# Stored factors staged in a weight slot, four plain pairs per stage, and the first squares summed by POOL in a residual block kernel

## The chip, the cores and the metric

One program runs on one core of one Trainium2 chip. The metric is device microseconds for one execution; the median over the executions shown is compared. The engines that matter are PE (TensorE, matmuls, with PEld its weight loads), DVE (VectorE), ACT (ScalarE), POOL (GpSimd) and SP (SyncE), whose queue issues the DMAs in order.

## What is computed

```python
def reference(x, ...):
    x = x + 0.5 * swiglu(rmsnorm(x, norm_ffn1), ffn1_wg, ffn1_wu, ffn1_wd)
    h = rmsnorm(x, norm_mix)
    x_m, z_m, x_r, y_r = split(h @ w_in)
    out_m = mlstm_group(x_m, z_m, ...)      # 4 heads, chunkwise matrix memory
    out_r = rglru_group(x_r, y_r, ...)      # 4 block-diagonal groups, conv and scan
    x = x + concat[rmsnorm(out_m), rmsnorm(out_r)] @ w_out
    x = x + 0.5 * swiglu(rmsnorm(x, norm_ffn2), ffn2_wg, ffn2_wu, ffn2_wd)
    return rmsnorm(x, norm_final)

def swiglu(x, wg, wu, wd):
    return (silu(x @ wg) * (x @ wu)) @ wd
```

There are 1024 tokens and 1024 channels, the inner width of each SwiGLU is 2816 (22 rows of 128), and everything is float32.

## The kernel before

Tokens lie along the free dimension, channels along the 128 partitions. x is transposed: eight row tiles of 128 channels by 1024 tokens, each in two halves of 512 tokens. Every matmul operand is split into a high and a low part (`split`: a cast by ACT, line 111, and a subtraction by DVE, line 112), and each product is made of three matmuls (high by high, high by low, low by high), so one 128-deep step on 512 tokens is three matmuls of 512 columns.

**The two FFN stages** (`ffn`) bear the change. Each has 22 pairs of a gate row and an up row. The first `PLAIN` = 3 pairs are computed plainly: `plain(h, f)` makes, for one half of the tokens, 24 matmuls for the gate and 24 for the up product, so a pair costs 96 over both halves. They read `hT`, the split but not yet normalized x. From pair 3 on, a pair is one object `Pair`, which forms a two by two block product with seven block products of 12 matmuls each (84 in all), the last of them from the tile `wd`. That scheme needs sums of weight blocks (`Pair.sums`, POOL, lines 520 to 523) and sums of blocks of normalized x (`Mixed`: `normalize` line 381, `combine` line 388, `operand`). The seven factors B11, T1, T2, B21, T3, B22, T4 are split tiles called `bop`. `Mixed` is a list of fifteen steps, one of which is popped after each half of a `plain`; what is left is popped when a product asks for it.

The down projection uses the same scheme for rows 0 to 15 of the inner width: two groups of eight rows, each with seven `Stored` factors which `Sink` wrote to DRAM (`f_d`) while the gate and up pairs ran, and four `Pair`s per group. So the factors change twice in a stage: from the last gate and up pair to group 0, and from the last pair of group 0 to group 1. The last pair before such a change makes the next factors ready: `after(i)`, called behind block product i, calls `Stored.get` for factor i (two loads of 512 KB into `raw` tiles, two splits) and then `Pair.prepare(i)` for the next pair (loads, sums, splits). Rows 16 to 21 are multiplied plainly at the end.

**Buffers.** `rawp` has four tiles of 4 KB per partition for what comes from DRAM; a pair before the change holds four of them (g, u, s, z). `wup` has four slots of 8 KB per partition with the tag `wu` for split weights; a pair holds three (wg, ws, wz), and its fourth product operand wu lies in `wd`. `bigp` has six tiles for hT, x and the last four factors; `bx` has three for the first three factors. In an FFN stage the eight PSUM banks are one pool `B`. `rb_late` holds the reciprocal root of the mean square of each token, spread over all partitions; its last use in a stage is in the plain pairs and in `normalize`.

**The start.** Before the first FFN, for each half and row, x is loaded (SP), split and scaled into hT by ACT and DVE (lines 115 and 116), and squared. The squares of one row are summed over channels by PE: `square_on_pe` squares into a `t2` tile (ACT, line 248) and adds four float32 matmuls of two columns (line 250, eight records) to a PSUM bank. `rstd_of` makes the root (POOL, line 144), and `spread` (line 175 on PE, from tiles that DVE makes in line 172) puts it into `rb_late`. In the second FFN the last products of the output projection feed `Norm.feed`, where the squares are summed by POOL (line 187), with DVE for the last row, and `row_rstd` (line 152) sums over partitions on PE.

**Order.** The order on the engines is that of the program text, except that the tile framework issues an instruction once its buffers are free. What is to come later is written with `defer(n, fn)`: `fn` runs at the n-th `tick`, and there is a tick behind each `project_half`, each `project_halves`, each group of `products` and each block product. The plain part of an FFN runs in the order (half, pair): (0,0), (0,1), (1,0), then their finishes, (1,1), the first gate and up pair's loads, sums and two splits, (0,2), finishes, (1,2), two more splits.

## Time and profile before

| what | value |
|---|---|
| median of 3 runs | 2184.8 us (2182.94 to 2188.53) |
| the profiled execution, its own time | 2185.25 us |
| its span, first to last instruction | 2183.5 us |
| PE busy | 2095.9 us (96%) |
| DVE, ACT, POOL busy | 1230.9, 872.5, 735.6 us |
| share of the chain that ended last: PE, DVE, DMA, POOL | 74%, 10%, 6%, 4% |

PE is busy nearly throughout, but the busy time of a matmul is no measure of its rate: a matmul of 512 columns is shown as some 390 ns long while the next one starts 227 ns later. What is lost is therefore read from how many matmuls start in a stretch, and from the idle time in front of a matmul with its releaser in the brackets.

### The profile page before, as it was taken

Reading aid. Unit: us, or ns where it says so; the run is one execution under the profiler, and the core shown is the slowest. Engines: PE = TensorE matmul, PEld = TensorE weight load, DVE = VectorE, ACT = ScalarE, POOL = GpSimd, SP = SyncE. Lnnn points to the kernel's source line nnn. Section 1 sums busy time; section 2 is a strip of 40 time slices with the busy share of each in tenths; the row PEclk is TensorE's granted clock in tenths of the full one; section 3 lists DMA queues with packets and bytes.
Section 4 is the critical chain, followed back from the end, with each engine's and each line's share of the span. In section 5 each row is a group of like instructions: output and inputs, shape, how many; then the busy total and the mean of one; then the engine's idle time right before and its main releaser. Section 6 shows DMA issues by size and latency. Waiting matters only on the chain.

```text
span 2183.5 us, 25040 instructions
## 1 busy us (share of the span) xinstructions
PE 2095.9 (96%) x9618; PEld 1727.3 (79%) x9618; DVE 1230.9 (56%) x1682; ACT 872.5 (40%) x1183; POOL 735.6 (34%) x496
## 2 busy tenths in 40 slices
PE   8989999999899999999999999998999999989898
PEld 7778888877688788878778888776788888867687
DVE  4853333355663545675537998878733333365654
ACT  4343333342432345564546554233433333342333
POOL 1355555323222302232311122423554554233303
PEclk9999999999999999999999999998999999999999
DMA  3243222243442312122146332121433322253432
GB/s 137 77 172 108 102 102 105 78 169 101 164 157 72 122 39 68 65 90 103 68 144 223 106 107 71 56 98 47 144 131 101 107 102 101 88 172 104 138 106 78
DMA packets 98368, 236.08 MB, mean 108 GB/s; under 512 B 9412, under 2 KB 28100, under 8 KB 97224
## 3 DMA queue, kind: packets, MB, share of 16 engines
q1 hardware_dynamic: 98248, 234.48, 31.5%
q8 instruction: 75, 1.23, 0.2%
q14 instruction: 45, 0.37, 0.1%
HBM read 168.89 MB, written 65.55 MB: 107 GB/s over the span
## 4 chain that ended last, share of the span: by engine, by line
PE 74%; DVE 10%; DMA 6%; POOL 4%; ACT 3%; issue 3%; SPq 0%; POOLq 0%; DVEq 0%; ACTq 0%
PE bank_b L445 39%; PE bank_a L327 12%; PE bank_b L344 8%; PE bank_s L344 3%; PE bank_b L327 2%; DVE bop L112 2%; PE bank_a L893 2%; PE bank_b L320 2%; DVE wu L112 1%; PE bank_s L1170 1%; PE bank_b L1199 1%; DMA raw<-in_db_dram 1%; DVE xs L1324 1%; DMA raw<-f_d0B 1%; DMA raw<-f_d1B 1%
## 5 line engine op out<-in xcount | busy, mean ns | idle before, releaser
L445 PE MATMUL bank_b<-bop,wu 128*128 128x512 f32 x3888 | 902.5, 392 | 30.4 <-DVE xs L642 12.8
L445 PEld LDWEIGHTS bank_b<-bop,wu 128*128 128x128 f32 x3888 | 733.7, 189 | 190.4 <-issue 11.0
L112 DVE TENSOR_TENSOR wu<-raw,wu 128x1024 fp32r<-128x1024 f32 (+1 forms) x233 | 297.4, 1278 | 425.9 <-ACT wu L111 425.8
L111 ACT CAST wu<-raw 128x1024 fp32r<-128x1024 f32 (+1 forms) x233 | 242.9, 1046 | 378.7 <-PE bank_b L445 230.0
L327 PE MATMUL bank_a<-hT,wu 128*128 128x512 f32 x1488 | 345.7, 391 | 3.1 <-ACT t L921 1.4
L327 PEld LDWEIGHTS bank_a<-hT,wu 128*128 128x128 f32 x1488 | 277.9, 188 | 64.1 <-POOL hT L112 1.9
L520 POOL TENSOR_TENSOR raw<-raw 128x512 f32<-128x512 f32 x54 | 76.4, 1415 | 517.6 <-DMA raw<-in_up_dram 292.4
L445 PE MATMUL bank_b<-bop,wd 128*128 128x512 f32 x648 | 159.6, 394 | 11.1 <-DVE ct L614 4.4
L344 PE MATMUL bank_b<-u,wu 128*128 128x512 f32 (+1 forms) x768 | 162.6, 364 | 1.5 <-DVE xs L1324 0.8
L610 ACT COPY ct<-bank_b 128x512 f32<-128x512 f32 x114 | 67.0, 587 | 230.3 <-PE bank_b L445 230.3
L445 PEld LDWEIGHTS bank_b<-bop,wd 128*128 128x128 f32 x648 | 121.9, 189 | 40.8 <-issue 5.4
L344 PEld LDWEIGHTS bank_b<-u,wu 128*128 128x128 f32 x768 | 131.8, 189 | 26.6 <-DVE xs L1324 2.5
L327 PE MATMUL bank_b<-hT,wu 128*128 128x512 f32 x528 | 124.9, 395 | 4.2 <-DVE wu L112 2.5
L614 DVE TENSOR_TENSOR ct<-ct,bank_b 128x512 f32<-128x512 f32 x114 | 78.0, 684 | 83.0 <-PE bank_b L445 83.0
L327 PEld LDWEIGHTS bank_b<-hT,wu 128*128 128x128 f32 x528 | 99.5, 190 | 25.9 <-DVE wu L112 3.4
L187 POOL TENSOR_TENSOR acc<-acc,t 128x512 f32<-128x512 f32 (+1 forms) x40 | 50.0, 1250 | 177.0 <-ACT t L185 176.3
L642 DVE SCALAR_TENSOR_TENSOR xs<-bank_b,xs 128x512 f32<-128x512 f32 x112 | 76.8, 686 | 53.9 <-PE bank_b L445 53.5
L344 PE MATMUL bank_s<-wu 128*128 128x512 f32 x384 | 97.8, 395 | 1.8 <-ACT wu L111 1.1
L112 DVE TENSOR_TENSOR bop<-raw,bop 128x1024 fp32r<-128x1024 f32 x56 | 70.3, 1264 | 41.0 <-ACT bop L111 40.9
L858 DVE SCALAR_TENSOR_TENSOR t<-bank_a,ch,t 128x1023 f32<-128x1023 f32 (+2 forms) x48 | 61.3, 1278 | 46.3 <-ACT t L855 45.8
L344 PEld LDWEIGHTS bank_s<-wu 128*128 128x128 f32 x384 | 69.5, 188 | 17.2 <-DVE wu L112 2.1
L111 ACT CAST bop<-raw 128x1024 fp32r<-128x1024 f32 x56 | 58.5, 1051 | 60.6 <-DMA raw<-f_d1T 28.3
(245 smaller groups left out, 2580.7 us busy)
## 6 DMA issues: line engine op xcount, KB each, us to landing
raw<-in_up_dram SPq DMA_DIRECT2D x87, 512.0 KB, 3.5
raw<-in_db_dram SPq DMA_DIRECT2D x32, 512.0 KB, 4.1
raw<-in_win_dram SPq DMA_DIRECT2D x32, 512.0 KB, 3.5
xs<-in_xT_dram SPq DMA_DIRECT2D x32, 256.0 KB, 6.0
raw<-f_d0T SPq DMA_DIRECT2D x16, 512.0 KB, 4.9
raw<-f_d1T SPq DMA_DIRECT2D x16, 512.0 KB, 4.8
x_d<-xs SPq DMA_DIRECT2D x32, 256.0 KB, 2.0
v_d<-u SPq DMA_DIRECT2D x8, 1024.0 KB, 3.9
```

What stands on the lines that cost most here:

```text
L111: nc.scalar.copy(hi, src)
L112: (eng or nc.vector).tensor_tensor(out=lo, in0=src, in1=hi.bitcast(F32), op=ALU.subtract)
L187: eng.tensor_tensor(out=box[0], in0=box[0], in1=sq, op=ALU.add)
L320: nc.tensor.matmul(ps, lhsT=w[:, a, k * P:(k + 1) * P], rhs=hT[b][half][:, k], start=(k == 0 and n == 0), stop=(k == NK - 1 and n == 2))
L327: nc.tensor.matmul(ps, lhsT=w[:, a, k * P:(k + 1) * P], rhs=hT[b][half][:, k], start=(k == 0 and n == 0), stop=(k == NK - 1 and n == 2))
L344: nc.tensor.matmul(ps, lhsT=w[:, a, m * P:(m + 1) * P], rhs=u[:, b, pieces[h]], start=(i == 0 and n == 0), stop=(i == len(lhs) - 1 and n = ...
L445: nc.tensor.matmul(ps, lhsT=w[:, a, k * P:(k + 1) * P], rhs=u[:, b, k], start=(first and k == 0 and n == 0), stop=(k == 3 and n == 2), ski ...
L520: add(out=self.s[:, lo], in0=self.u[:, lo], in1=self.u[:, hi], op=ALU.add)
L610: nc.scalar.copy(c, ps)
L614: nc.vector.tensor_tensor(out=t[a], in0=t[a], in1=ps, op=ALU.add)
L642: nc.vector.scalar_tensor_tensor(out=xt, in0=ps, scalar=0.5, in1=xt, op0=ALU.mult, op1=ALU.add)
L858: nc.vector.scalar_tensor_tensor(out=y[:, s:], in0=ps[:, :T - s], scalar=chan(f"{name}c{3 - s}", c), in1=y[:, s:], op0=ALU.mult, op1=ALU.add)
```

## The change

1. `square_on_pe` goes, with the constant `ones2`. The start calls `norm.square` instead: ACT squares a row into a `t2` tile, POOL adds it to an accumulator (DVE the last row), and `row_rstd` and `spread` follow at later ticks. In the second FFN the spread of the first half comes one tick later (5 for 4).
2. `Stored.get` no longer loads. `fetch(i)` loads factor i: an even one with one DMA of 1 MB into a slot of the weights' tag `wu`, an odd one with two of 512 KB into a `raw` tile and into a tile that shares `rb_late`'s buffer. `split(i)` splits it. Factors 0 and 1 are fetched ahead of the last pair's products, factor i + 2 behind the split of factor i.
3. `Pair.sums` keeps only s in a tile of its own: z is written over the low half of u and, later (`last_sum`), over the high half of g. A pair holds three `raw` tiles. `split_z` splits the two halves one by one.
4. `PLAIN` is 4. The first pair's loads, sums and splits are spread behind (0,3), (1,2) and (1,3).

```diff
-                self.square(xs, m, h, (4, 2)[h], (4, 1)[h])
+                self.square(xs, m, h, (5, 2)[h], (4, 1)[h])
...
-        def square_on_pe(self, xs, m, h, wait):
-
-            if m == 0:
-                self.acc[h] = bank_b()[:, 0:8]
-                nc.tensor.matmul(self.acc[h], lhsT=ident, rhs=ones2[:, 2:10], start=True, stop=True)
-            sq = t2(self.pool)
-            nc.scalar.activation(sq, row(xs, m)[:, half_of(h)], AF.Square)
-            for t in range(4):
-                nc.tensor.matmul(self.acc[h][:, 2 * t:2 * t + 2], lhsT=sq[:, t * P:(t + 1) * P],
-                                 rhs=ones2[:, 0:2], start=False, stop=(m == NK - 1),
-                                 skip_group_check=True)
...
+        def fetch(self, i):
+            if i >= len(FACTORS):
+                return
+            src = self.src[FACTORS[i]].rearrange("p a n -> p (a n)")
+            if i % 2 == 0:
+                r = wup.tile([P, 2, T], R32, tag="wu", name="stage", bufs=4).bitcast(F32)
+                nc.sync.dma_start(out=r.rearrange("p a n -> p (a n)"), in_=src)
+                self.raw[i] = [r[:, 0], r[:, 1]]
+            else:
+                self.raw[i] = [raw_tile(), self.late.tile([P, T], F32, tag="rb_late", name="stage",
+                                                          bufs=1)]
+                for c, r in enumerate(self.raw[i]):
+                    nc.sync.dma_start(out=r, in_=src[:, c * T:(c + 1) * T])
+
+        def split(self, i):
+            t = self.ops[FACTORS[i]] = factor_tile(self.bx, FACTORS[i])
+            for c, r in enumerate(self.raw.pop(i)):
+                split(t[:, 0, 2 * c:2 * c + 2], t[:, 1, 2 * c:2 * c + 2],
+                      r.rearrange("p (a n) -> p a n", a=2))
 
         def get(self, name):
-            if name not in self.ops:
-                t = self.ops[name] = factor_tile(self.bx, name)
-                for c in range(0, 4, 2):
-                    r = load(self.src[name][:, c:c + 2].rearrange("p a n -> p (a n)"))
-                    split(t[:, 0, c:c + 2], t[:, 1, c:c + 2],
-                          r.rearrange("p (a n) -> p a n", a=2))
             return self.ops[name]
...
-    PLAIN = 3
+    PLAIN = 4
...
         def sums(self):
-            self.s, self.z = raw_tile(), raw_tile()
+            self.s = raw_tile()
             lo, hi = half_of(0), half_of(1)
             add = nc.gpsimd.tensor_tensor
             add(out=self.s[:, lo], in0=self.u[:, lo], in1=self.u[:, hi], op=ALU.add)
             add(out=self.s[:, hi], in0=self.s[:, lo], in1=self.g[:, lo], op=ALU.subtract)
-            add(out=self.z[:, lo], in0=self.g[:, lo], in1=self.u[:, lo], op=ALU.subtract)
-            add(out=self.z[:, hi], in0=self.g[:, hi], in1=self.s[:, hi], op=ALU.subtract)
+            add(out=self.u[:, lo], in0=self.g[:, lo], in1=self.u[:, lo], op=ALU.subtract)
+
+        def last_sum(self):
+
+            hi = half_of(1)
+            nc.gpsimd.tensor_tensor(out=self.g[:, hi], in0=self.g[:, hi], in1=self.s[:, hi],
+                                    op=ALU.subtract)
...
-            self.wz = weights(None, loaded=self.z)
+            self.wz = wup.tile([P, 2, T], R32, tag="wu", name="wu", bufs=4)
+            for r, sl in ((self.u, half_of(0)), (self.g, half_of(1))):
+                split(self.wz[:, 0, sl], self.wz[:, 1, sl], r[:, sl])
...
-            {0: self.load, 1: self.sums, 2: self.split_g, 4: self.split_s, 5: self.split_z,
-             6: self.split_u}.get(i, lambda: None)()
+            (self.load, self.sums, self.split_g, self.last_sum, self.split_s, self.split_z,
+             self.split_u)[i]()
...
                 late = [plain(1, 1)]
-                p.load()
-                p.sums()
-                p.split_g()
-                p.split_s()
                 late.append(plain(0, 2))
                 for f in late:
                     f()
+                plain(0, 3)()
+                p.load()
+                p.sums()
                 plain(1, 2)()
+                p.split_g()
+                p.last_sum()
+                p.split_s()
+                plain(1, 3)()
                 p.split_z()
                 p.split_u()
...
                         if nxt[1] is not factors:
-                            nxt[1].get(FACTORS[i])
+                            nxt[1].split(i)
+                            nxt[1].fetch(i + 2)
                         nxt[0].prepare(i)
+                    if nxt and nxt[1] is not factors:
+                        nxt[1].fetch(0)
+                        nxt[1].fetch(1)
                     p.run(factors.get, out, after)
...
-            norm.square_on_pe(xs, m, h, (3, 5)[h])
+            norm.square(xs, m, h, 2, (2, 3)[h])
```

## Rows read from the trace of the kernel before

**Rows 1.** Timeline of PE in steady pairs: start, us, engine, line, operation, tiles, count.
```profile
204.36 2.88 PE L445 MATMUL bank_b<-bop,wd 128*128 128x512 f32 x12
...
223.40 2.88 PE L445 MATMUL bank_b<-bop,wd 128*128 128x512 f32 x12
```

**Rows 2.** Windows: stretch, length, busy (instructions) by engine, granted clock, DMA share, GB/s.
```profile
10.50:57.30 46.80, 46.80 (x209) 40.74 (x210) 19.78 (x27) 18.52 (x30) 8.74 (x6) 1.00 0.30 113
57.30:130.90 73.60, 65.65 (x282) 53.55 (x281) 66.39 (x63) 30.80 (x36) 29.12 (x15) 0.95 0.28 99
454.60:525.00 70.40, 62.72 (x253) 48.88 (x252) 43.09 (x45) 28.75 (x32) 24.20 (x16) 0.95 0.46 157
544.10:613.20 69.10, 60.12 (x254) 48.02 (x253) 43.73 (x48) 25.71 (x26) 19.94 (x14) 0.98 0.43 145
1477.40:1582.30 104.90, 91.79 (x387) 74.28 (x387) 80.79 (x83) 38.57 (x47) 44.77 (x25) 0.92 0.26 92
1906.00:1976.40 70.40, 60.65 (x254) 47.82 (x253) 43.15 (x45) 28.81 (x32) 24.29 (x16) 0.98 0.46 157
1995.40:2064.70 69.30, 60.38 (x253) 47.90 (x252) 43.85 (x48) 25.72 (x26) 19.45 (x14) 0.98 0.44 144
```

**Rows 3.** Groups of lines in 0 to 60 us: count, busy us, mean ns, idle before.
```profile
L250 PE MATMUL bank_b<-ones,t 128*128 128x2 f32 x128 | 21.5, 290 | 4.5 <-ACT t L248 4.5
...
L248 ACT ACTIVATE t<-xs 128x512 f32<-128x512 f32 x16 | 10.0, 626 | 18.4 <-PE bank_b L250 18.4
```

**Rows 4.** Timeline of PE in the start and the first plain pairs.
```profile
24.17 4.19 PE L320 MATMUL bank_b<-hT,wu 128*128 128x512 f32 x9
...
57.50 0.62 PE L175 MATMUL bank_b<-t,ones_r 128*128 128x512 f32 x2
57.95 11.06 PE L327 MATMUL bank_b<-hT,wu 128*128 128x512 f32 x48
...
82.64 21.62 PE L327 MATMUL bank_b<-hT,wu 128*128 128x512 f32 x94 [1.81 <-DVE wu L112]
...
115.84 12.52 PE L445 MATMUL bank_b<-bop,wu 128*128 128x512 f32 x48 [6.14 <-ACT ct L610]
```

**Rows 5.** Timeline at the start of the second FFN.
```profile
1459.36 10.27 POOL L187 TENSOR_TENSOR acc<-acc,t 128x512 f32<-128x512 f32 x6 [36.06 <-ACT t L185]
...
1462.21 1.18 DVE L116 SCALAR_TENSOR_TENSOR hT<-xs,ch,hT 128x512 fp32r<-128x512 f32 x1
...
1487.69 0.79 PE L175 MATMUL bank_b<-t,ones_r 128*128 128x512 f32 x1 [9.85 <-DVE t L172]
...
1489.24 0.74 DVE L116 SCALAR_TENSOR_TENSOR hT<-xs,ch,hT 128x512 fp32r<-128x512 f32 x1
1489.37 0.79 PE L175 MATMUL bank_b<-t,ones_r 128*128 128x512 f32 x1 [0.89 <-DVE t L172]
...
1489.96 13.14 PE L320 MATMUL bank_b<-hT,wu 128*128 128x512 f32 x48
...
1502.95 0.95 PE L152 MATMUL bank_b<-ones_r,acc 128*128 128x2 f32 x8
...
1544.24 0.73 PE L327 MATMUL bank_b<-hT,wu 128*128 128x512 f32 x2 [1.67 <-ACT wu L111]
```

**Rows 6.** Groups of lines in 454.4 to 525 us, the first change of factors: xcount, busy us, mean ns, idle before.
```profile
L112 DVE TENSOR_TENSOR bop<-raw,bop 128x1024 fp32r<-128x1024 f32 x14 | 17.4, 1253 | 12.4 <-ACT bop L111 12.4
L111 ACT CAST bop<-raw 128x1024 fp32r<-128x1024 f32 x14 | 14.6, 1052 | 11.3 <-DMA raw<-f_d0T 8.2 <-DMA raw<-f_d0B 3.1
L111 ACT CAST wu<-raw 128x1024 fp32r<-128x1024 f32 x9 | 9.4, 1048 | 21.1 <-POOL raw L521 10.9 <-PE bank_b L445 4.3 <-POOL raw L523 3.0
...
L642 DVE SCALAR_TENSOR_TENSOR xs<-bank_b,xs 128x512 f32<-128x512 f32 x13 | 8.9, 683 | 3.6 <-PE bank_b L445 3.6
```

**Rows 7.** The page, part 6: DMA issues, KB each, us from issue to landing.
```profile
raw<-f_d0T SPq DMA_DIRECT2D x16, 512.0 KB, 4.9
...
v_d<-u SPq DMA_DIRECT2D x8, 1024.0 KB, 3.9
```

More of the change, by code (lines that the diff above doesn't have):

```diff
@@ L59, in hymba_block_kernel @@
     ones = ones_r.bitcast(F32)
-    ones2 = const.tile([P, 64], F32, name="ones2")
-    nc.vector.memset(ones2[:, 0:2], 1.0)
-    nc.vector.memset(ones2[:, 2:10], 0.0)
     mhalf = const.tile([P, 1], F32, name="mhalf")
@@ L425, in hymba_block_kernel, with __init__ @@
     class Stored:
[L428 to L437 removed]
+        def __init__(self, bx, late, src):
+            self.bx, self.late, self.src, self.ops, self.raw = bx, late, src, {}, {}
+        def fetch(self, i):
[16 more added lines that the diff above has]
+                      r.rearrange("p (a n) -> p a n", a=2))
+        def get(self, name):
             return self.ops[name]
@@ L648, in ffn @@
                 for g in range(BLOCKED // 8):
-                    factors = Stored(bx, f_d[g])
+                    factors = Stored(bx, norm.pool, f_d[g])
                     work += [(Pair(pool, blocked[g, 2 * j], blocked[g, 2 * j + 1]), factors, down(j))
```

6 lines of the change are left out of this document (removed).

## The prediction

> **What bounds the kernel now.** PE does. First the steady stretch: two last block products of neighbouring pairs start 19.04 us apart [rows 1], so 84 matmuls of 512 columns take 0.2267 us each, and nothing is lost. Then the windows [rows 2], in which the reader should compare the length with the matmuls that the code puts there. In 10.5 to 57.3 us there are 96 such matmuls (21.8 us) in 46.8. In 57.3 to 130.9 there are 192 plain ones and the first pair's 84 (62.6 us) in 73.6; in 1477.4 to 1582.3 the second FFN's 288 and 84 (84.3 us) in 104.9. Each change of factors covers three pairs (57.1 us), and the four windows take 70.4, 69.1, 70.4 and 69.3 us: 279.2 against 228.5, so 50.7 lost, 12.7 each. Elsewhere the change touches only the steady pairs. So some 97 us are within reach, and each stretch has its own late engine.
>
> At the start, 128 records of the squares' two-column matmuls take 21.5 us of PE, and ACT stands 18.4 us in front of squares for PE to free a tile [rows 3]: PE is what the others wait for. Its 512-column matmuls start 0.43 us apart there (nine in 4.19 us), the spacing of the lower clock of 1.2 GHz (the clock column says 1.00 in the window, but the spacing decides), against 48 in 11.06 us later at 2.4 GHz [rows 2, 4]. In the plain pairs PE stands 1.81 us for the third pair's weights and 6.14 us in its first block products, DVE being busy 66.4 of 73.6 us [rows 2, 4]; the granted clock falls to a mean of 0.95 with these stops. In the second FFN PE stands 9.85 and then a little longer in front of the spread, whose tiles DVE makes late, and 1.67 us later on for weights [rows 5]. At a change of factors ACT stands 11.3 us for the stored factors' DMAs and 13.9 us for POOL's sums in front of weights; DVE in turn stands 12.4 us for ACT [rows 6].
>
> **The start, part by part.** The 128 records go from PE, and with them the breaks between row products. The 96 matmuls cost 21.8 us, plus a slow beginning: after the stop in the second FFN 48 matmuls took 13.14 us where 48 take 11.06 [rows 4, 5], 2.1 us more. The first `row_rstd` now stands among them: 0.95 us [rows 5]. Sum 24.8 against 46.8: 22.0 less. This needs the others to keep up. ACT and DVE are busy 18.5 and 19.8 us in the old window [rows 2], less than the new one's 24.8, and the second half of hT is needed only when (1,0) begins, behind all 96. POOL gets twelve adds that the start does not have; the nearest row is the same sum in the second FFN, six in 10.3 us [rows 5], 1.71 us each, 20.5 in all. They end before (1,0) needs their result; I price them at nothing and keep 0 to 3 us. `t2` has three buffers, so behind a late add ACT's next square waits, and behind that the next row's split.
>
> What DVE loses beside POOL: a split of 128x512 (line 116) took 1.18 us beside line 187 and 0.74 alone [rows 5]; sixteen times 0.44 is 7 us, and 27 us of DVE still fit into the 35.7 before (1,0)'s last rows.
>
> The Trainium skill (SBUF — State Buffer, section "Who interferes with whom") says that a VectorE instruction with two SBUF inputs and a GpSimd instruction that reads SBUF exclude each other, the later one blocking fully until the first ends. These rows show a lengthening of 0.44 us, not the 1.71 us of an add; by the rule as written the twelve adds could put 20.5 us on DVE, not 7, and the sum would be that of the third rival; by the rows it stays.
>
> **Four plain pairs.** From the 96th matmul the first FFN now has 288 plain ones until its first block pair is due, where before 192 and a pair of 84 stood: 65.3 us, with two spreads of 0.45 (57.50 to 57.95) and one `row_rstd` of 0.95 [rows 4, 5]: 67.1 against 73.6. The twelve matmuls more are 2.7 us, contained in this. The old waits should go: the weights of pairs 2 and 3 find free slots one unit of 10.9 us ahead, and of `Mixed`'s fifteen steps three are left, not six, when the first block product starts; the factors they make are wanted 13.6 us later. DVE has about its old 66 us of work in 67, so I allow 1.5 us (bounds 0 and 6.1, the old stall kept). POOL's finishes and sums of stored rows fit (29.1 us of 73.6, rows 2). Start and plain pairs: 22.0 + 6.5 - 1.5 = 27.0 less; bounds 20 and 30.
>
> **The second FFN.** 384 matmuls, 87.1 us, with 1.9 for spreads and `row_rstd`: 89.0. The first half's spread comes one tick later, so 48 matmuls (10.9 us) stand ahead of the instruction that PE used to wait at. DVE's second tile was there at 1489.4 [rows 5]; PE now gets there at 1477.4 + 10.9 = 1488.3. I allow 2 us there and 1 for the rest: 92.0 against 104.9, 12.9 less. What could still hold PE at 1477.4 are PSUM banks that DVE has yet to read, in the same DVE queue, at most some 6 us; bounds 7 and 15.5.
>
> **The changes of factors.** The seven factors are 7 MB either way. Factors 0 and 1 now land ahead of the pair; later ones are asked for when their buffer's reader, the split two factors before, is done. A 1 MB load isn't in the trace as such: 512 KB of a factor landed in 4.9 us and a 1 MB store in 3.9 [rows 7]; I take 4.9 and keep 3.9 to 9.8 (two of the first). On SP a fetch waits for its buffer with the next pair's two loads behind it, and POOL's sums wait for those. The splits are not made cheaper. DVE has in such a pair fourteen times 1.25 us [rows 6], about 4.4 for the next weights and seven results of 0.68 [rows 6]: 26.7 us in a pair of 19.04. By hand, with casts on time, it begins 3.9 us into the pair; the fifth result, due at 16.3 for the seventh product, is read at 17.6: 1.3 us lost. If everything that is left then comes ahead of the next pair's first result, that is read at 30.2 where PE wants it at 25.7: 4.5 more. A late third factor (asked for at some 6.5 us, there at 11.4, wanted at 8.2) adds up to 3. The third pair's loss, from weights behind sums behind loads behind fourteen stored loads, goes, since fewer `raw` tiles are held. So 1.3 to 9 us, and I take 5.5 of the 12.7: 4 x 7.2 = 28.8 less; bounds 8 and 45.
>
> **Sums in place.** Each of the 52 pairs gets one cast and one subtraction more (two of 512 for one of 1024), a few tenths of a microsecond on ACT and DVE, idle over half of the steady time; nothing on PE.
>
> **Sum.** 27.0 + 12.9 + 28.8 = 68.7. The profiled execution took 2185.25 us, so 2116.5; the median of the runs is 0.45 lower: 2116.
>
> **Rivals.** *The staging moves the wait and removes little* (ACT and DVE, not the loads, are the limit, or the fetches find no free slot): the changes lose 11 us each. For it speak the 26.7 us of DVE and the single staging slot; against it, that ACT and DVE stand idle for DMAs now. Gain 27.0 + 12.9 + 6.8 = 46.7: 2138. *The changes vanish nearly* (1.5 us each): gain 84.7, 2100. DVE's surplus speaks against it. *The start gives less*: PE stays at 1.2 GHz through (0,0), 48 times 0.20 us more than at the higher clock, 9.8 instead of 2.1, or each of POOL's adds holds DVE up for its whole 1.71 us, 19.8 + 20.5 = 40.3 us for the 35.7 there are, so that (1,0) waits 4.6: up to 2124. *Slower*: in all 52 pairs the weights come late, since u and g are now held until the last split of z, so that the next load, its sums on POOL and the split of s form one chain. The chain: u free at 1.4 us (two operations of 512 columns, 0.68 each as in rows 6), load 4.9, three sums of 1.71, cast and subtraction 2.3, ending at 13.7 us; it must end by 21.8 (19.04 and one product). Only where it is 8.1 us longer does a pair begin to lose, and only from 1.45 us of loss a pair (75 us in all) would the kernel be slower by 0.3%: 2192.
>
> **How the numbers follow.** A run of this kernel tells about 0.3% (6.5 us) from no change. Chances: forecast 0.58, staging of little use 0.20, changes vanish 0.10, start gives less 0.06, slower 0.03, something unnamed that eats all of it 0.03. The range from the bounds, without both far ends at once: 2096 to 2148. Faster by over 0.3%: 0.94; same: 0.03; slower: 0.03.
>
> **What would show it.** The first spread on PE near 41 us, not 57.5 (it stands 24 matmuls later than it did); PE's 512-column matmuls 0.227 us apart from about 15 us on; the first block pair near 103 us with no stop behind its second product; no stop of 9.9 us at the second FFN's start; windows of three pairs near 63 us at the changes, ACT's casts of `bop` no longer waiting for the DMA; steady pairs still at 19.04. Wrong would be: steady pairs over 19.1, casts that wait for the staged loads, or (1,0) waiting for hT.

## The result and the profile after

| | before | changed |
|---|---|---|
| median | 2183.9 us (4 runs, 2181.9 to 2188.5) | 2147.6 us (4 runs, 2143.7 to 2154.8) |
| ratio | 1 | 0.9835, 95% interval 0.9802 to 0.9868 |
| the profiled execution, its span | 2185.25, 2183.5 us | 2154.82, 2153.1 us |

The kernel became faster by 36.3 us where 68.7 were forecast (36.3 = 2183.9 - 2147.6). The way is right and the time lies within the range (at its upper end), but all three terms of the sum came out short: 14.3 to 15.6 for 27.0 (start and plain pairs), 8.0 to 10.1 for 12.9 (second FFN), 10.3 to 10.7 for 28.8 (changes). The page of the changed kernel, busy time by engine:

```profile
PE 2080.2 (97%) x9526; PEld 1711.5 (79%) x9526; DVE 1288.0 (60%) x1730; ACT 864.7 (40%) x1225; POOL 760.3 (35%) x502
```

PE's busy time fell by 15.7 us, but DVE's rose by 57; where 11 of them come from is shown further down.

To compare kernels, four stretches are read from PE's timeline, each between starts of last block products (`bop,wd` in the names), as in [rows 1]. "f = 5": from the start of the execution to that product of weight pair 5 in the first FFN. "Between": from that product of the first FFN's last pair to that of f = 5 in the second FFN. "Change 1" and "change 2": the seven pairs from the last undisturbed gate and up pair to the second stored pair of group 1, one stretch for each FFN with two changes of factors in it; without loss it is 7 x 19.04 = 133.3 us. Where the planner puts some matmuls of a pair ahead of others, single pairs shift and the seven do not. Undisturbed pairs are 19.04 us in every kernel here. Where an expectation below gives an end of f = 5, it is the start of that product's last matmul, 2.5 us later than in the table.

| kernel | ratio to before (95%) | f = 5 | between | change 1 | change 2 |
|---|---|---|---|---|---|
| before | 1 | 166.3 | 969.1 | 158.6 | 158.8 |
| forecast, in these stretches | 0.969 | 139.3 | 956.2 | 144.2 | 144.4 |
| changed, first profile | 0.9835 (0.9802 to 0.9868) | 152.0 | 961.1 | 154.1 | 152.9 |
| changed, second profile | 0.9840 (0.9813 to 0.9867) | 150.7 | 958.9 | 152.7 | 154.0 |
| e1 POOL squares alone | 0.9979 (0.9963 to 0.9995) | 161.4 | 969.7 | 157.4 | 159.7 |
| e2 three plain pairs | 0.9934 (0.9910 to 0.9958) | 159.3 | 971.7 | 151.8 | 151.7 |
| e3 old staging and sums | 0.9867 (0.9848 to 0.9885) | 147.0 | 955.2 | 155.3 | 156.3 |
| e4 late splits | 0.9776 (0.9759 to 0.9794) | 151.8 | 959.1 | 143.8 | 144.0 |
| e5 written order on PE | 0.9899 (0.9877 to 0.9921) | 148.8 | 958.5 | 158.8 | 158.1 |
| e6 = e4 and e5 | 0.9772 (0.9753 to 0.9792) | 149.4 | 955.7 | 143.8 | 143.7 |
| e7 = e4 and an order on POOL | 0.9742 (0.9715 to 0.9769) | 149.0 | 956.5 | 142.1 | 142.4 |
| e9 = e7 with own rows for z | 0.9740 (0.9722 to 0.9758) | 148.5 | 958.1 | 143.7 | 145.4 |
| e11 = e7 with five plain pairs | 0.9743 (0.9727 to 0.9759) | 144.5 | 958.4 | 145.4 | 143.9 |
| e13 = e3 with late splits | 0.9914 (0.9895 to 0.9932) | 148.4 | 955.9 | 160.8 | 159.9 |
| e14 = e7, five plain pairs, then four | 0.9701 (0.9655 to 0.9748) | 144.4 | 957.0 | 143.7 | 143.4 |

The stretches come from one profile each; the two profiles of the changed kernel differ by 1.1 to 2.2 us in a stretch, and less than that is not read from the table. A profile shows one execution and not the median one: both of the changed kernel were the slowest of their four, as were those of e4 and e9, and those of e3, e6, e7, e13 and e14 were the fastest of theirs.

**The start.** PE's timeline of the changed kernel: start, us, operation, count, idle time before and its releaser.

```profile
30.84 5.69 PE L308 MATMUL bank_b<-hT,wu 128*128 128x512 f32 x24
38.28 1.16 PE L149 MATMUL bank_b<-ones_r,acc 128*128 128x2 f32 x8 [1.75 <-DVE acc L184]
39.31 7.20 PE L308 MATMUL bank_b<-hT,wu 128*128 128x512 f32 x24
46.35 0.62 PE L172 MATMUL bank_b<-t,ones_r 128*128 128x512 f32 x2
...
108.45 3.33 PE L441 MATMUL bank_b<-bop,wu 128*128 128x512 f32 x14
...
116.53 12.82 PE L441 MATMUL bank_b<-bop,wu 128*128 128x512 f32 x48 [2.01 <-ACT ct L613]
130.78 3.02 PE L441 MATMUL bank_b<-bop,wd 128*128 128x512 f32 x12 [1.44 <-DVE ct L617]
133.64 11.04 PE L441 MATMUL bank_b<-bop,wu 128*128 128x512 f32 x48
146.46 5.74 PE L441 MATMUL bank_b<-bop,wu 128*128 128x512 f32 x24 [1.78 <-ACT ct L613]
152.03 2.88 PE L441 MATMUL bank_b<-bop,wd 128*128 128x512 f32 x12
```

The 96 matmuls that ended at 57.3 us [rows 2] end at 36.3 (30.84 and 24 times 0.2267). The spread is at 46.35, where 57.50 was [rows 4] and 41 was forecast. The first block pair takes 25.2 us (108.45 to 133.64) instead of 19.04: its third product waits for copies out of PSUM, its last for DVE (e9 shows why). From the spread to that pair it is 62.1 us, as forecast (41 to 103): the plain pairs themselves ran as expected, only later.

**The second FFN.**

```profile
1461.37 12.78 PE L301 MATMUL bank_b<-hT,wu 128*128 128x512 f32 x48 [2.00 <-DVE xs L1334]
1473.98 0.61 PE L172 MATMUL bank_b<-t,ones_r 128*128 128x512 f32 x2
...
1568.34 2.88 PE L441 MATMUL bank_b<-bop,wd 128*128 128x512 f32 x12
...
1584.31 7.35 PE L441 MATMUL bank_b<-bop,wu 128*128 128x512 f32 x24 [2.20 <-ACT ct L613]
1591.50 2.88 PE L441 MATMUL bank_b<-bop,wd 128*128 128x512 f32 x12
```

The stop of 9.85 us in front of the spread [rows 5] is gone as forecast (1473.98, no idle time). PE waits 2.00 us for PSUM banks that DVE has yet to read, the cost that the lower bound named, and the second block pair loses 4.1 us (23.16 us between the last products at 1568.34 and 1591.50).

**The changes of factors.** Groups of lines in 440.5 to 509.3 us: count, busy us, mean ns, idle before; the answer to [rows 6].

```profile
L109 DVE TENSOR_TENSOR bop<-stage,bop 128x1024 fp32r<-128x1024 f32 x11 | 15.5, 1437 | 3.1 <-ACT bop L108 3.1
L108 ACT CAST bop<-stage 128x1024 fp32r<-128x1024 f32 x11 | 11.0, 1045 | 0.5 <-DMA stage<-f_d0T 0.5
...
L109 DVE TENSOR_TENSOR bop<-raw,bop 128x1024 fp32r<-128x1024 f32 x3 | 4.8, 1583 | 0.8 <-ACT bop L108 0.8
```

ACT's casts wait 0.5 us for the stored factors' DMAs where they waited 11.3: the staging does what it says. DVE's idle time in front of these splits falls from 12.4 to 3.9 us. But PE still loses 10 us per change. The timeline of one:

```profile
469.61 3.42 DVE L109 TENSOR_TENSOR bop<-stage,bop 128x1024 fp32r<-128x1024 f32 x2
...
470.37 0.74 PE L441 MATMUL bank_b<-bop,wu 128*128 128x512 f32 x2 [1.14 <-ACT wu L108]
...
474.18 1.04 ACT L108 CAST wu<-raw 128x1024 fp32r<-128x1024 f32 x1 [3.86 <-POOL raw L517]
474.62 1.27 DVE L645 SCALAR_TENSOR_TENSOR xs<-bank_b,xs 128x512 f32<-128x512 f32 x2
...
475.28 10.62 PE L441 MATMUL bank_b<-bop,wu 128*128 128x512 f32 x37 [4.17 <-ACT wu L108]
```

PE stands 1.14 and 4.17 us in the first stored pair (4.87, 4.77 and 4.89 for the second stop at the other changes). Two things end at 475.3: a cast of the second stored pair's weights (474.18 to 475.22), for which PE waits because the planner has put three matmuls of that pair ahead of the first pair's third product; and DVE's L645, which reads the first product's result out of the bank that the third product needs, and which stands behind the splits of the last two factors. Which of the two counts is what the first experiments ask.

### The profile page after: what moved, and what is told of

Read it like the earlier page. It is cut to its first block, busy times and chain, and to the rows that moved or that the text cites. A ratio compares the mean times of both kernels' runs of the same rounds, so it can differ in the third digit from the quotient of the medians.

```text
span 2153.1 us, 24930 instructions
## 1 busy us (share of the span) xinstructions
PE 2080.2 (97%) x9526; PEld 1711.5 (79%) x9526; DVE 1288.0 (60%) x1730; ACT 864.7 (40%) x1225; POOL 760.3 (35%) x502
## 4 chain that ended last, share of the span: by engine, by line
PE 74%; DVE 10%; DMA 5%; issue 4%; ACT 3%; POOL 3%; SPq 0%; POOLq 0%; DVEq 0%; ACTq 0%
PE bank_b L441 38%; PE bank_a L308 13%; PE bank_b L325 8%; PE bank_b L308 4%; PE bank_s L325 3%; DVE wu L109 2%; PE bank_a L903 2%; DVE bop L109 2%; PE bank_s L1180 1%; PE bank_b L1209 1%; DMA raw<-in_up_dram 1%; DMA raw<-in_dn_dram 1%; DVE xs L1334 1%; DMA xs<-in_xT_dram 1%; DVE hT L113 1%
## 5 line engine op out<-in xcount | busy, mean ns | idle before, releaser
L441 PE MATMUL bank_b<-bop,wu 128*128 128x512 f32 x3744 | 874.9, 394 | 33.1 <-ACT wu L108 23.3
L441 PEld LDWEIGHTS bank_b<-bop,wu 128*128 128x128 f32 x3744 | 709.8, 190 | 189.8 <-ACT wu L108 26.8
L109 DVE TENSOR_TENSOR wu<-raw,wu 128x1024 fp32r<-128x1024 f32 (+1 forms) x283 | 329.1, 1178 | 334.7 <-ACT wu L108 334.1
L516 POOL TENSOR_TENSOR raw<-raw 128x512 f32<-128x512 f32 x52 | 73.4, 1411 | 450.8 <-DMA raw<-in_up_dram 288.5
L308 PE MATMUL bank_b<-hT,wu 128*128 128x512 f32 x720 | 166.9, 392 | 1.0 <-DVE wu L109 1.0
L308 PEld LDWEIGHTS bank_b<-hT,wu 128*128 128x128 f32 x720 | 136.0, 189 | 29.8 <-DVE wu L109 1.4
L441 PE MATMUL bank_b<-bop,wd 128*128 128x512 f32 x624 | 150.3, 390 | 1.9 <-DVE ct L617 1.4
L441 PEld LDWEIGHTS bank_b<-bop,wd 128*128 128x128 f32 x624 | 116.9, 188 | 27.1 <-DVE ct L617 1.9
L184 POOL TENSOR_TENSOR acc<-acc,t 128x512 f32<-128x512 f32 (+1 forms) x52 | 68.2, 1312 | 195.6 <-ACT t L182 194.3
L645 DVE SCALAR_TENSOR_TENSOR xs<-bank_b,xs 128x512 f32<-128x512 f32 x112 | 76.7, 687 | 95.4 <-PE bank_b L441 95.3
L523 POOL TENSOR_TENSOR raw<-raw 128x512 f32<-128x512 f32 x52 | 78.2, 1504 | 36.1 <-DVE wu L109 36.1
L325 PEld LDWEIGHTS bank_s<-wu 128*128 128x128 f32 x384 | 69.5, 188 | 17.4 <-DVE wu L109 2.1
L518 POOL TENSOR_TENSOR raw<-raw 128x512 f32<-128x512 f32 x52 | 81.4, 1566 | 0.0
```

The costliest lines, as they stand in the source:

```text
L109: (eng or nc.vector).tensor_tensor(out=lo, in0=src, in1=hi.bitcast(F32), op=ALU.subtract)
L184: eng.tensor_tensor(out=box[0], in0=box[0], in1=sq, op=ALU.add)
L308: nc.tensor.matmul(ps, lhsT=w[:, a, k * P:(k + 1) * P], rhs=hT[b][half][:, k], start=(k == 0 and n == 0), stop=(k == NK - 1 and n == 2))
L325: nc.tensor.matmul(ps, lhsT=w[:, a, m * P:(m + 1) * P], rhs=u[:, b, pieces[h]], start=(i == 0 and n == 0), stop=(i == len(lhs) - 1 and n = ...
L441: nc.tensor.matmul(ps, lhsT=w[:, a, k * P:(k + 1) * P], rhs=u[:, b, k], start=(first and k == 0 and n == 0), stop=(k == 3 and n == 2), ski ...
L516: add(out=self.s[:, lo], in0=self.u[:, lo], in1=self.u[:, hi], op=ALU.add)
```

## The experiments

**e4, the last two splits later.** In the changed kernel, the splits of B22 and T4 move from the last gate and up pair into the first stored pair.

```diff
+                        if i < 2 and held:
+                            held.pop(0)()
...
-                            nxt[1].split(i)
+                            if i < 5:
+                                nxt[1].split(i)
+                            else:
+                                held.append(lambda st=nxt[1], k=i: st.split(k))
```

> The changed kernel with the last two splits of each set of stored factors (B22 and T4) put behind the first and the second product of the first stored pair instead of the last two of the pair before. In the changed kernel PE stands 1.1 and then 4.2 to 5.1 us in that pair at each change, at half clock behind it. Theory of two waits that end together: VectorE's queue (the result of the first product behind the splits) and TensorE's order (three matmuls of the second stored pair stand ahead of the third product and wait for a cast that depends on late loads): this edit takes away the first wait alone, so the stall stays within 1 us, 2143 to 2149 us. Rival, VectorE's queue alone: the stall of 4.2 to 5.1 goes at all four changes with the half clock behind it, 5 to 7 us each, 2120 to 2128 us. Rival, TensorE's order alone: no change, 2148 us.

Measured: 2131.65 us, 0.9776. The stretches of the changes fall from 153.4 (the mean of the changed kernel's four) to 143.9 us, 4.8 us per change: the rival of VectorE's queue alone, a little short of its 5 to 7. DVE reads the first product's result at 466.61 us there, not at 474.62, with the last gate and up pair ending at the same time within 0.3 us. **e5, the written order on PE**, each block product behind the last matmul of the one before:

```diff
+            if last[0] is not None:
+                order.enter_context(tc.issue_after(last[0]))
```

> The changed kernel with TensorE's block products held in the order in which they are written (each behind the last matmul of the product before), so that no matmul of the second stored pair stands ahead of the first pair's third product. Theory of two waits that end together: the third product still waits for VectorE to add the first product's result (it ended at 475.3 us where the stall ended at 475.3), so at most 1 us per change, 2143 to 2149 us. Rival, TensorE's order alone: the 4.2 to 5.1 us and the half clock go at each change, 2120 to 2128 us. Rival, VectorE's queue alone: no change, 2148 us.

Measured: 2158.19 us, 0.9899: slower than the changed kernel, 158.4 instead of 153.4 us per two changes. **e6, both edits:**

> The late splits and the written order together. Theory of two waits: only here do the stalls of 1.1 and 4.2 to 5.1 us go, with the half clock behind them: 5 to 7 us at each of four changes, 2120 to 2128 us. Rivals of one wait: the same as the better of the two runs with one edit. Rival, late loads of the second stored pair (its sums' input lands 468.3 and 470.1 us): the stall moves to the second product of the second stored pair and little is gained, 2140 to 2148 us.

Measured: 2131.39 us, 0.9772, changes 143.7 us, as with the late splits alone. PE's timeline of e5 and then of e4:

```profile
461.19 5.61 PE L444 MATMUL bank_b<-bop,wu 128*128 128x512 f32 x24
472.06 13.67 PE L444 MATMUL bank_b<-bop,wu 128*128 128x512 f32 x48 [5.25 <-DVE xs L649]
```

```profile
462.79 14.91 PE L441 MATMUL bank_b<-bop,wu 128*128 128x512 f32 x64
480.47 3.01 PE L441 MATMUL bank_b<-bop,wd 128*128 128x512 f32 x12 [2.77 <-DVE xs L645]
```

My theory of two waits that both have to go has fallen, and so has the one on PE's order. With the order held, PE stands just as long at the third product, now openly for DVE's reading of the result (L649 is line 645 there), and the matmuls that the planner had put into the gap come later: the planner's order had filled the gap, not made it. With DVE's queue relieved, the 64 matmuls from 462.79 on run through without a stop there, with the planner's order as before. What is left is mainly the stop of 2.8 us at the seventh product and 1.3 us in the last gate and up pair (22.65 us, but with 94 matmuls in it: the planner has put ten of the next pair there, which fill part of its wait for DVE; with the order held, in e6, it loses 3.4).

**e3, old staging and sums**, that is `Stored.get` and `Pair.sums` as before, with POOL squares and four plain pairs:

> The changed kernel with the old loading of the stored factors (each in two rows, loaded when it is split) and the old weight sums (four raw rows per pair); the POOL squares and four plain pairs stay. Measured so far: the changed kernel 2147.6 us, its loss per change of factors 9.4, 11.5, 10.1 and 9.6 us (40.5 in all) where before has 12.7 each (50.7). If the staging gives these 10.2 us: losses back to about 12.7 each, 2158 us. If it is of no use and the gain at the changes comes with the plain pairs or by chance: 2148 us. If the staging also costs something at the start (the sums in place, in the first two block pairs): the stretch up to the end of the second block pair is 1 to 3 us shorter than the changed kernel's 154.5.

Measured: 2151.52 us, 0.9867. The interval overlaps with that of the changed kernel, so by the times the staging with its sums in place brings 0.3% or nothing. The stretches say more, though e3's come from its fastest execution: the changes take 155.8 on average, only 2.4 us more than with staging (1.2 per change, not 2.5), while f = 5 comes 3.7 to 5.0 us earlier and "between" is 3.7 to 5.8 shorter without the sums in place. Of the f = 5 difference up to 2.0 is an earlier spread (44.32); 3.0 to 3.7 lies behind the spread. So staging by itself is worth little, and the start did pay for something that comes with it, somewhat more than the 1 to 3 us expected.

**e13, late splits on old staging:**

```diff
-                            nxt[1].get(FACTORS[i])
+                            if i < 5:
+                                nxt[1].get(FACTORS[i])
+                            else:
+                                held.append(lambda st=nxt[1], k=i: st.get(FACTORS[k]))
```

> The changed kernel with old loading of the stored factors and old sums, as run before (ratio 0.9867; 155.3 and 156.3 us for the seven pairs around two changes, 133.3 without loss), and with the last two factors of each set loaded and split in the first stored pair. With staging these late splits brought 153 us to 143.9. Theory that VectorE's surplus is the larger part of the loss and the loads the smaller: 146 to 150 us each here, ratio 0.980 to 0.983. Rival, the splits help only where the loads are early (staging needed): 154 us and more, 0.986. Rival, the loads are no cost at all: 144 us, 0.977.

Measured: 2162.71 us, 0.9914; worse than all three theories' times, with the changes where the rival that the splits need the staging put them (154 us and more). The same late splits that bring 9.5 us per two changes with staging cost 4.6 without. In the groups of e13 from 437 to 508 us, with two rows of its timeline behind them, and then in those of e4:

```profile
L108 ACT CAST bop<-raw 128x1024 fp32r<-128x1024 f32 x14 | 14.6, 1052 | 11.9 <-DMA raw<-f_d0T 7.9 <-DMA raw<-f_d0B 4.0
...
480.28 1.04 ACT L108 CAST bop<-raw 128x1024 fp32r<-128x1024 f32 x1 [3.06 <-DMA raw<-f_d0T]
...
481.38 0.51 PE L426 MATMUL bank_b<-bop,wd 128*128 128x512 f32 x1 [1.88 <-ACT bop L108]
```

```profile
L108 ACT CAST bop<-stage 128x1024 fp32r<-128x1024 f32 x11 | 11.0, 1047 | 0.0
```

Two changes take (mean of both FFNs):

| | splits early | splits late |
|---|---|---|
| old loads and sums | 155.8 | 160.4 |
| staged loads, sums in place | 153.4 | 143.9 |

So the loads and DVE's surplus take turns. Early splits with late loads: DVE waits for loads. Early loads with early splits: DVE is full, and the result of the first stored product waits in its queue. Late splits with late loads: the load of a factor is asked for only in the pair that needs it, and the seventh product waits for it (1.88 us). Only both together take the loss from 11.2 us per change (e3; 12.7 in the kernel before, and no run here separates the 1.5 between them) to 5.3, the size that the forecast gave the staging alone.

**e1, the POOL squares alone**, put into the kernel before:

```diff
-            norm.square_on_pe(xs, m, h, (3, 5)[h])
+            norm.square(xs, m, h, 2, (2, 3)[h])
```

> The kernel before with one part of the change alone: the start's squares are summed by POOL instead of TensorE. In the changed kernel the first 96 matmuls are done at 36.3 us instead of 57.3, but the pair f = 5 ends only 14.2 us earlier. Theory that VectorE's work bounds the stretch behind (it was busy 66.4 of 73.6 us there in the kernel before): the 21 us are there at 36 us and partly given back at the first block products: the pair f = 5 ends 10 to 15 us earlier than 168.8 us, the stops of 1.8 and 6.1 us that the kernel before has are as long or longer; 2169 to 2174 us. Rival, the plain pairs are what falls short and the squares bring all they promised: f = 5 ends 20 to 22 us earlier; 2158 to 2163 us.

Measured: 2177.73 us, 0.9979; f = 5 comes 4.9 us earlier, less than either theory said. PE's timeline, and below it the windows up to the end of the first block pair:

```profile
42.99 1.87 PE L152 MATMUL bank_b<-ones_r,acc 128*128 128x2 f32 x8 [6.02 <-DVE acc L187]
44.72 7.91 PE L327 MATMUL bank_b<-hT,wu 128*128 128x512 f32 x24
52.47 0.62 PE L175 MATMUL bank_b<-t,ones_r 128*128 128x512 f32 x2
...
97.79 5.60 PE L445 MATMUL bank_b<-bop,wu 128*128 128x512 f32 x24
...
114.94 8.55 PE L445 MATMUL bank_b<-bop,wu 128*128 128x512 f32 x24 [5.01 <-ACT ct L610]
```

```profile
10.50:36.60 26.10, 24.77 (x100) 18.62 (x99) 24.96 (x20) 18.62 (x32) 19.08 (x14) 1.00 0.49 189
36.60:97.80 61.20, 52.31 (x207) 42.16 (x206) 48.03 (x53) 17.20 (x20) 24.28 (x16) 0.86 0.20 69
97.80:125.80 28.00, 22.20 (x84) 17.47 (x83) 24.19 (x22) 13.21 (x17) 12.98 (x6) 0.88 0.48 160
```

The 20.7 us are there at 36.6, and all but 4.9 of them are given back by 125.8. The key is the spread: DVE's work for the block products (`Mixed`) can begin only behind it. It moved from 57.50 to 52.47, 5.0 us, and f = 5 moved by 4.9. From the spread to f = 5 it is 108.8 us in the kernel before, 108.9 in e1 and 109.1 in e2: in these three kernels that distance is fixed, and what PE saves ahead of the spread counts only as far as the spread itself comes earlier. It came only 5.0 us earlier because PE stood 6.02 us for the accumulator: DVE's last add to it meets the first pair's three sums on POOL (rows in "Why DVE was fuller than counted").

**e2, three plain pairs** in the changed kernel, with `(4, 2)` for `(5, 2)` and the first pair's loads and sums behind (1,1) again:

> The changed kernel with three plain pairs as before (and the order and the wait of the kernel before around them); POOL squares, staging and sums in place stay. Theory that VectorE's work bounds the stretch: with three plain pairs the same work of VectorE falls on 12 matmuls fewer and the sums' operands come earlier, so f = 5 ends 3 to 8 us later than in the changed kernel (158 to 163 us), and in the second FFN likewise; 2155 to 2163 us. Rival, the fourth plain pair only moves the stops: within 2 us, about 2148 us.

Measured: 2168.06 us, 0.9934: f = 5 7.3 to 8.6 us later than in the changed kernel, "between" 10.6 to 12.7 longer. The fourth plain pair, with the later place of the first pair's sums, works twice. It shortens the distance from the spread to f = 5 from 109.1 to 105.7 and 106.4 us; and the spread itself comes 3.9 and 5.9 us earlier, since PE's stop for the accumulator (6.02 us in e1, 5.35 in e2) is 1.75 and 0.54 us where the sums no longer run beside the last squares. The two make up about half of what start and plain pairs brought.

**The changed kernel again**, no edit:

> The changed kernel itself, to have it beside the other edits on one chip and a second profile of it. Expected as measured before: 0.9835 of the kernel before, about 2143 us where that takes 2179; the sixth weight pair (f = 5) ends near 154.5 us, the four changes of factors take 66 to 69 us each. If the start differs by more than 2 us from the first profile, that much of any difference at the start says nothing.

Measured: 2149.74 us, 0.9840. f = 5 differs by 1.3 us between the profiles.

**e7, an order on POOL**: with late splits, and a pair's three sums held behind the activation product (line 632) of the pair before.

```diff
+            with ExitStack() as order:
+                if pooled[0] is not None:
+                    order.enter_context(tc.issue_after(pooled[0]))
+                add(out=self.s[:, lo], in0=self.u[:, lo], in1=self.u[:, hi], op=ALU.add)
...
+                            pooled[0] = getattr(mul, "ins", mul)
```

> The version with the last two splits of each set of factors put into the first stored pair (its stall of 4.2 to 5.1 us per change went, 0.9776 of the kernel before), with one thing more: on POOL each pair's three weight sums are held behind the product of activations of the pair before. In the changed kernel the second block pair of each FFN loses 2.1 and 4.1 us: a copy out of PSUM waits 8.2 us for a buffer that this product frees, and the product stands in POOL's queue behind sums that wait 11.4 us for their load. If that queue is the cause, both losses go (19.04 us for the pair) and the first block pair keeps its loss: 3 to 6 us less than that version, 2124 to 2128 us. Rival, VectorE's backlog is the cause there too: the second pair keeps 1 to 4 us, 2130 us.

Measured: 2127.63 us, 0.9742. POOL and ACT in the second block pair of the changed kernel, then POOL of e7:

```profile
140.14 1.29 POOL L516 TENSOR_TENSOR raw<-raw 128x512 f32<-128x512 f32 x1 [11.38 <-DMA raw<-in_up_dram]
...
144.00 1.30 POOL L632 TENSOR_TENSOR even<-ct 128x512 f32<-128x512 f32 x1
...
145.33 1.07 ACT L613 COPY ct<-bank_b 128x512 f32<-128x512 f32 x2 [8.18 <-POOL even L632]
```

```profile
129.52 1.49 POOL L637 TENSOR_TENSOR even<-ct 128x512 f32<-128x512 f32 x1 [3.37 <-issue]
...
137.55 1.28 POOL L521 TENSOR_TENSOR raw<-raw 128x512 f32<-128x512 f32 x1 [6.55 <-DMA xs<-in_xT_dram]
```

The product now runs 8 us ahead of the sums and the second pair has no stop; in the second FFN "between" is 956.5, and its second pair takes 19.1 us. In the first FFN the first block pair keeps its loss (26.4 us).

The wait is there as the theory has it, and other profiles without this order show its size. The later the next pair's load lands, the longer PE stands in the second FFN's second pair: 2.20 us where POOL's sums begin 9.7 us behind the first pair's last product (changed, first profile), 1.47 at 8.9 (e4), 0.96 at 8.4 (changed, second profile), and nothing at 7.2 (e6, "between" 955.7). So the order makes the pair independent of when the load lands, but how much it gains in the time isn't shown: e6 does without it, the second pair of the first FFN has no stop in the changed kernel's second profile either, and the intervals of e7 (0.9742) and of e4 and e6 (0.9776, 0.9772) overlap.

**e9, own rows for z** in the first three block pairs (part of the edit below), and **e11, five plain pairs**, with the first pair's loads and sums behind (1,3), both on e7:

```diff
...
+            if self.own:
+                self.z = raw_tile()
+                add(out=self.z[:, lo], in0=self.g[:, lo], in1=self.u[:, lo], op=ALU.subtract)
+                add(out=self.z[:, hi], in0=self.g[:, hi], in1=self.s[:, hi], op=ALU.subtract)
+                return
...
```

> The version with late splits and the held order on POOL (0.9742 of the kernel before, f = 5 ended at 151.5 us), and for the first three block pairs of each FFN the sums not in place but in a row of their own, as before the change; from the fourth block pair on in place. With old sums and old staging f = 5 ended at 149.5 us and the second FFN's start took 126.9 where the changed kernel takes 129.8 and 132.6. Theory that the sums in place cost at the start because z's second sum and its splits in halves come later and hold POOL, ACT and VectorE in the busy first pairs: 1 to 2 us less at f = 5, nothing in the second FFN, which has nothing left to lose; 0.973. Rival, all of it was the order on POOL: no change at all, 0.974.

> The version with late splits and the held order on POOL, with five plain pairs instead of four. There the first block pair of the first FFN still takes 25.9 us instead of 19.04, that of the second 18.9. Theory that VectorE is behind with work and only needs time in which TensorE is busy with plain matmuls: the first FFN's f = 5 pair ends 1 to 4 us earlier than 151.5 (12 matmuls more are 2.7 us, against some 7 us of stops), the second FFN's start gets 2.7 us longer; 2125 to 2130 us where that version takes 2127.6. Rival, the stops move along with the first block pair: 2.7 us longer in both, 2133 us.

Measured: e9 2126.21 us, 0.9740, the time of e7, and f = 5 only 0.5 us earlier. But the spread of e9's profile stood 2.9 us later (46.66 for 43.75; the 24 matmuls ahead of it took 7.30 us for 5.70). From the spread to f = 5 it is 101.9 us, and 105.2 in e7. So it is in every profile with four plain pairs: 101.9 to 102.7 with z in a row of its own (e9, e3, e13), 104.9 to 106.4 with z in place (changed twice, e4 to e7). Writing z in place does cost the start of the first FFN some 3 us, with POOL's order held or not. The chain in e7, and then the same sum and product in e9:

```profile
124.89 1.26 POOL L528 TENSOR_TENSOR raw<-raw 128x512 f32<-128x512 f32 x1
126.18 0.62 ACT L108 CAST wu<-raw 128x512 fp32r<-128x512 f32 x1 [5.78 <-POOL raw L528]
126.83 0.69 DVE L109 TENSOR_TENSOR wu<-raw,wu 128x512 fp32r<-128x512 f32 x1 [4.30 <-ACT wu L108]
...
128.18 4.25 PE L441 MATMUL bank_b<-bop,wd 128*128 128x512 f32 x12 [3.07 <-DVE ct L622]
```

```profile
118.30 2.26 POOL L526 TENSOR_TENSOR raw<-raw 128x512 f32<-128x512 f32 x1
...
129.48 2.88 PE L441 MATMUL bank_b<-bop,wd 128*128 128x512 f32 x12
```

In place, z's second sum (L528) can be made only when g has been split, and then stands on POOL behind three sums of stored rows (`Sink`). Its cast waits 5.78 us for it and DVE 4.30 us for the cast, and DVE's reading of a product (L622, at 127.44) stands behind that split: the first block pair's seventh product waits for it. In a row of its own the sum is made ahead of those three, and the product doesn't wait. The measured times can't tell 3 us (0.15%). e11 2125.99 us, 0.9743. Its first block pair:

```profile
128.19 16.48 PE L441 MATMUL bank_b<-bop,wu 128*128 128x512 f32 x72
144.51 2.88 PE L441 MATMUL bank_b<-bop,wd 128*128 128x512 f32 x12
```

19.04 us without a stop, and f = 5 4.5 us earlier (from the spread 100.2), though it costs 12 matmuls more; in the second FFN, which had nothing to lose, "between" is 1.9 us longer. The work behind the spread only needed the time; that it is DVE's alone isn't shown, since the chain above runs over POOL and ACT too. **e14** takes five plain pairs in the first FFN and four in the second (`PLAIN` becomes an argument of `ffn`):

> Late splits and the held order on POOL, with five plain pairs in the first FFN (f = 5 ended at 147.0 us with five, at 151.5 with four) and four in the second (its start took 129.6 us with five, 127.0 with four). If the two starts stand for themselves, f = 5 ends near 147, the second start takes near 127, and the time is 2.7 us under the version with five in both: 2122 to 2124 us, 0.972 to 0.973. If the changes of factors or the second start vary from one build to the next by as much as that, 0.974 as before.

Measured: 2124.79 us, 0.9701 (0.9655 to 0.9748): f = 5 at 144.4, "between" 957.0. It is the fastest profile here (span 2120.8 us), but from e7, e9 and e11 it can't be told by the measured times: 2.7 us would be 0.12%.

## Why the prediction was half right

**POOL squares, 22.0.** The removed PE time was right: 21.0 us at the 96th matmul, with stops of 1 to 2 us. The step that failed is to enter this sum as a gain at the end of the stretch. PE was the late engine up to 57 us, but behind that DVE was, from the spread on; alone the squares are worth 4.9 us (e1). The text had asked whether DVE and ACT keep up inside the 24.8 us and not what DVE has to do behind the spread, and it placed the spread at 41 us by counting matmuls ahead of it; what it waits for is the accumulator that POOL and DVE finish. In the changed kernel it stood at 46.35 and 44.33, 5.4 and 3.3 us late.

**Four plain pairs, 6.5 less 1.5.** Too small as a term of its own (7.3 to 8.6 at f = 5 between e2 and the changed kernel), too large in the sum. The allowance for DVE was the mis-sized number: the first block pair loses 6.1 us in the first profile and 8.6 in the second (27.6 us to the next pair's first matmul), for 1.5. That it comes to 108.45 and not 103 is the late spread alone. Together start and plain pairs brought 14.3 to 15.6 for 27.0, below the bounds of 20 to 30. e11 shows that the work behind the spread lacked time: with 21.8 us more of plain matmuls the loss is gone. Some 3 us of it were z in place (e9).

**Why DVE was fuller than counted.** From 10.5 us to the end of the first block pair DVE was busy 86.2 us before [rows 2] and 97.2 in e1 (24.96 + 48.03 + 24.19): 11.0 us more, of which two additions, 1.4 us by their 0.68 alone, are new work. The prediction allowed 7 for the twelve adds beside the hT splits, and none for those behind them. The splits kept to that (13.0 us before, 20.1 in e1, 14 of them in the stretch); the rest was the part priced at nothing. One place in e1's timeline shows how it comes about (the fence after this one is the same 128x4 subtraction in the changed kernel, with POOL idle):

```profile
37.27 1.71 POOL L521 TENSOR_TENSOR raw<-raw 128x512 f32<-128x512 f32 x1
37.78 1.22 DVE L164 TENSOR_TENSOR parts<-r,parts 128x4 fp32r<-128x4 f32 x1
...
38.94 1.78 POOL L522 TENSOR_TENSOR raw<-raw 128x512 f32<-128x512 f32 x1
39.52 1.75 DVE L116 SCALAR_TENSOR_TENSOR hT<-xs,ch,hT 128x512 fp32r<-128x512 f32 x1
40.68 1.70 POOL L523 TENSOR_TENSOR raw<-raw 128x512 f32<-128x512 f32 x1
41.19 1.74 DVE L187 TENSOR_TENSOR acc<-acc,t 128x512 f32<-128x512 f32 x1
```

```profile
36.22 0.15 DVE L161 TENSOR_TENSOR parts<-r,parts 128x4 fp32r<-128x4 f32 x1
```

0.15 us becomes 1.22, ending 0.02 us behind POOL's sum; 0.75 becomes 1.75; the two engines alternate. The Trainium skill (SBUF — State Buffer, section "Who interferes with whom") says that a VectorE instruction with two SBUF inputs and a GpSimd instruction that reads SBUF exclude each other until the first ends. These rows agree with it, and the mean lengthening of 0.44 us in [rows 5], which I weighed against it, hid that: with adds of 1.71 us from 1459.36 on, the split that began at 1462.21 and took 1.18 for 0.74 can have met only the rest of one. What it costs in all is still not the 20.5 us worked out by the rule (9.6 us more in e1, if all that is not new work is put down to it), since not every DVE instruction meets one on POOL.

**The second FFN, 12.9.** Measured 8.0 and 10.1. The spread's stop went, the wait for PSUM banks was the 2 us in the bounds, and what is missing was lost in the second block pair. Where the second block pair had no stop it was 12.6 (e7, with the order on POOL) and 13.4 (e6, without it). The step that failed is one that wasn't there: POOL's queue, in which the sums of the next pair, waiting for their load, hold up the product that frees a buffer for the copies, by 0 to 2.2 us according to when the load lands.

**The changes, 28.8.** Measured 10.3 and 10.7: 10.1 us are lost per change, not 5.5. The mechanism that the text gave is the one found (the loads come on time, then the result of the first stored product is read too late), and the rival that the staging only moves the wait is what happened (it put the loss at 11 and the chance at 0.20). The number that was off is the time at which that result is read: 30.2 us into the change by hand, where PE wants it at 25.7; in the trace 34.9 (475.28 - 440.35). The 14 splits of 1.25 us took 1.44 and 1.58 each, 20.3 us for 17.4, which is 2.9 of the 4.7 us; two of them and the split of wd (1.74 us) lie beside POOL's sums just ahead of L645. The 5.5 that the text took was near its schedule's 1.3 + 4.5; what was measured lies above its upper end of 9.

**Sums in place, 0.** Steady pairs are 19.04, the chain of the slower rival never shows. At the start the term was not nothing but some 3 us in the first FFN (e9, e3, e13): the text counted the casts and subtractions that are added, and not that the second sum comes late in POOL's queue. In the second FFN the second pair, which loses 4.1 and 1.3 us in the changed kernel, loses nothing with z in rows of its own (19.04 in e3, e9 and e13).

**A sum of the text.** "Some 97 us within reach" is 107 by its own four differences (25.0, 11.0, 20.6 and 50.7); nothing else was worked out from it.

**What stays open.** In e7 some 4.5 us are still lost per change, 1.3 of them in the last gate and up pair. The first block pair takes 25.2, 27.6, 26.4 and 23.5 us in two profiles of the changed kernel, e7 and e3. In the first three its last product starts 22.3 us behind its first, and only the pace of that product's twelve matmuls differs (3.0, 5.5 and 4.3 us, at a mean granted clock of 1.00, 0.50 and 0.69); why the clock differs is not settled.

## What to carry to other kernels

When work is taken off the bounding engine, ask from which event on the next engine's chain runs, and move the end of the stretch by how much that event moves, not by the time saved ahead of it. Where a late load and a full engine hide each other, neither edit alone shows its worth: loads staged early brought 1.2 us per change, later splits alone cost 2.3, both together brought 5.9. And read each in-order queue for what stands behind an instruction that waits: here a product on POOL behind sums that waited for a DMA cost up to 4 us in the second FFN, and a sum that could only be made late, because it was written over its own input, cost 3 us at the end of a chain of three engines.

## What the runs showed of the hardware that was not expected

PE's rate after a stop differs: behind a stop of 1.75 us at 38.28 the next 24 matmuls took 7.20 us in the changed kernel, and behind one of 1.77 us at 37.82 in e11 they took 5.75. The mean granted clock was 0.79 from 38.2 to 46.4 us in the one and 1.00 from 37.7 to 44.4 us in the other. The stop of 4.17 us at a change was followed by 37 matmuls in 10.62 us, 2.2 more than 37 x 0.2267, with a mean granted clock of 0.77 from 471 to 486 us.
